# One stage of a streaming-encoder kernel: the conditioning product turned round, with the weights as the stationary side

## The chip, the cores and the metric

The kernel runs on one core of a Trainium2 chip. Such a core has a matrix engine (PE, with its weight loads shown apart as PEld), a vector engine (DVE), a scalar engine (ACT), a third elementwise engine (POOL) and a queue engine (SP) that issues the DMA transfers. Each engine works through its own list of instructions in order; semaphores tie the lists together. The metric is the device time of one execution in microseconds.

## The reference

One layer of an encoder takes a prompt of 4096 frames and a sample of 64 frames, 1024 features wide. Each of the two sequences has one conditioning vector `c`. What matters here is the head of the layer:

```python
mod = jnp.einsum('bd,de->be', c, w_ada) + b_ada
shift, scale, gate = jnp.split(mod, 3, axis=-1)
h = rms_norm(x, g_pre) * (1 + scale[:, None]) + shift[:, None]
p = jnp.einsum('btd,de->bte', h, w_in)
```

`w_ada` is 1024 x 3072, so the shift and the scale need its first 2048 columns, 8 MB in float32. They have to be known, for a block of 128 features, before that block of `h` can be formed, and `h` is what every projection with `w_in` reads. Behind the projections come two chunked recurrences (GLA and HGRN2, four heads each), a gate, an output projection and a last norm. All inputs and outputs are float32.

## The kernel before

The prompt is cut into 16 groups of 256 frames. Features lie on the partitions, in `KT` = 8 blocks of 128. To keep float32's accuracy in products of the faster `float32r` type, each operand is split into a high and a low part (`split`: ACT casts to `hi`, DVE subtracts to `lo`), and a product is made of three: high by high, high by low, low by high.

The change touches `first_group` (line 220), which works on group 0 while the weights still arrive. Its order is written by hand (`manual_schedule`); behind it a list scheduler places the instructions, so what stands there moves when something ahead of it changes. `first_group` does this:

- Six and then eight products of zeros run first (`warm`). The two tiles of x are normed and turned (`turn(0)`, `turn(1)`, line 313), and small rows (conditionings, biases, gains) are loaded into `rows` and turned into the columns of `col` (lines 302 and 325).
- For each of the eight blocks k, `ada_load` (line 207) issues four transfers of 256 KB: the columns of `w_ada` that give shift (e = 0) and scale (e = 1) of block k. `ada_split` cuts them into `ada_h` and `ada_l` (lines 93 and 94). `ada_sum` (line 239) multiplies them: the stationary side is `c4`, four columns (both conditionings, high and low), the moving side 256 columns of `ada_h` or `ada_l`. The sum has four rows and lies in bank `o` of PSUM; `ada_out` (line 249) copies it out by ACT, and `ada_turn` (lines 257 to 262) turns it by PE into columns and adds high, low and bias on DVE into `md`.
- `modulate` (lines 273 to 277) makes the parts of `h` for block k from `md`: ACT the high part `hh`, DVE the low one.
- The loop over k then takes twelve products for q and k (line 356, tiles `hh` and `wa`) and twelve for the gate z (line 625, tiles `wv` and `hh`). In iteration k, the sum for block k+1 stands behind the first eight of the q-k products, and `modulate(k+1)` behind the last four.
- The weights `w_in` come by `first_load`, in a tile `e` (q and k) and half a tile `wst` (z). `weights` loads and splits the next piece, `w_v` (tiles `wb`), of which every third low part is made by POOL.

Behind the first group come the products with `wb` (line 625), the exponentials of z (lines 1112 to 1114), the transposes of a small tile `at` (line 1129), the norm and transposes of group 1's x (lines 491, 496, 547) and group 1's q-k products (line 613).

Of the kernel before, what the change touches and what calls it, by code (L numbers as in the profile page):

```python
# [6 lines left out]
F32 = mybir.dt.float32  # L7
F32R = mybir.dt.float32r
# [20 lines left out]
class Kernel:  # L29
# [177 lines left out]
    def ada_load(self, ap, k, few=()):  # L207

        sts = []
        for i in range(2):  # L210
            st = ap.tile([P, 4, 2, P], F32, name="ada_st", bufs=5)
            for e in range(2):
                src = self.t["w_ada"][0, i * 512 : i * 512 + 512, e * D + k * P : e * D + (k + 1) * P]
                self.nc.sync.dma_start(st[:, :, e, :], src.rearrange("(n p) c -> p n c", p=P))
                for dst, src in few[2 * i + e : 2 * i + e + 1]:
                    self.nc.sync.dma_start(dst, src)
            sts.append(st)
        return sts

    def first_group(self, ap, ada, w, rows):  # L220


        nc, col = self.nc, self.col
        W = self.W1
        T = GROUP
        parts = {}

        def ada_split(st):
            hi = ap.tile([P, 4, 2, P], F32R, name="ada_h", bufs=3)
            lo = ap.tile([P, 4, 2, P], F32R, name="ada_l", bufs=3)  # L230
            self.split(hi, lo, st)
            return hi, lo

        def ada_sum(pa, parts, steps):


            for m, i in steps:
                for n in range(4):
                    nc.tensor.matmul(
                        pa, self.c4[:, 4 * i + n, :], parts[i][m][:, n],  # L240
                        start=m + i + n == 0, stop=(m, i, n) == (1, 1, 3),
                    )

        def ada_bank():
            return self.ps("o")[:4, : 2 * P]

        def ada_out(pa):
            am = self.etile()[:4, : 2 * P]
            nc.scalar.copy(am, pa)
            return am  # L250

        all_steps = [(0, 0), (0, 1), (1, 0), (1, 1)]

        def ada_turn(k, am):
            pt = self.ps("ms")
            for e in range(2):
                nc.tensor.transpose(pt[:, 4 * e : 4 * e + 4], am[:, e * P : (e + 1) * P], self.ident[:4, :4])
            md = self.md[:, :, k, :]
            nc.vector.tensor_reduce(
                md, pt[:, :8].rearrange("p (e m c) -> p e c m", e=2, m=2), mybir.AxisListType.X, ALU.add  # L260
            )
            nc.vector.tensor_tensor(
                md, md, col[:, 16:32].rearrange("p (e k) -> p e k", e=2)[:, :, k : k + 1].to_broadcast([P, 2, 2]), ALU.add
            )

        def gain(k):
            return col[:, 32 + k : 33 + k]

        def modulate(k):
            sh, gs = self.sh[:, k, :], self.gs[:, k, :]  # L270
            u = self.h0[k // 2][:, :, k % 2]
            hf = self.hf[k // 2][:, k % 2]
            nc.scalar.activation(u[:, 0], hf, AF.Identity, bias=sh[:, 0:1], scale=gs[:, 0:1])
            nc.vector.tensor_scalar(hf, hf, gs[:, 0:1], sh[:, 0:1], ALU.mult, ALU.add)
            nc.vector.tensor_tensor(u[:, 1], hf, u[:, 0].bitcast(F32), ALU.subtract)

            nc.vector.tensor_scalar(gs, gs, gain(k), None, ALU.mult)

        def raw(k, eng):

            dst, src = self.hf[k // 2][:, k % 2], pts[k // 2][:, k % 2]
            if eng is nc.scalar:
                nc.scalar.activation(dst, src, AF.Copy, scale=gain(k))
            else:
                nc.vector.tensor_scalar(dst, src, gain(k), None, ALU.mult)

        def w_split(i, w):
            W[("qk", "z")[i]].append(self.split_w(w[i], ("wa", "wv")[i]))

        zero = self.ep.tile([P, 512], F32R, name="zero", tag="e", bufs=5)  # L290
        nc.gpsimd.memset(zero.bitcast(F32), 0.0)
        ws, sts = [w], [ada, self.ada_load(ap, 1)]

        pqk = [self.ps("pj") for _ in range(2)]

        def warm(n):
            for _ in range(n):
                nc.tensor.matmul(pqk[0], zero[:, :P], zero, start=True, stop=True)

        warm(6)  # L300
        pr = self.ps("ms")
        nc.tensor.transpose(pr[:, :16], rows[:16], self.ident[:16, :16])
        warm(8)
        self.x_norm(0, [0])
        nc.vector.tensor_copy(col[:, :16], pr[:, :16])
        self.x_norm(0, [1])
        cT = col[:, 0:16].rearrange("p (s k) -> p k s", s=2)
        self.split(self.c4[:, :, 0:2], self.c4[:, :, 2:4], cT)
        pts = [self.ps(n).rearrange("p (k t) -> p k t", k=2) for n in ("tp", "at", "at", "pj")]

        def turn(j):
            for k in range(KT):
                nc.tensor.transpose(
                    pts[k // 2][:, k % 2, j * P : (j + 1) * P], self.xs[j][:, k * P : (k + 1) * P], self.ident
                )

        turn(0)
        pa = ada_bank()
        parts[0] = [ada_split(sts[0][0])]
        ada_sum(pa, parts[0], [(0, 0)])  # L320
        turn(1)
        parts[0].append(ada_split(sts[0][1]))
        ada_sum(pa, parts[0], [(0, 1)])
        pr = self.ps("ms")
        nc.tensor.transpose(pr[:, :52], rows, self.ident[:52, :52])
        ada_sum(pa, parts.pop(0), [(1, 0), (1, 1)])
        self.hf = [self.hp.tile([P, 2, T], F32, name="hf", bufs=4) for _ in range(4)]
        nc.vector.tensor_copy(col[:, 16:], pr[:, 16:52])
        nc.vector.tensor_scalar(col[:, 24:32], col[:, 24:32], 1.0, None, ALU.add)
        raw(0, nc.scalar)  # L330
        w_split(0, ws[0])
        am = ada_out(pa)
        ws.append(self.first_load(1))
        sts.append(self.ada_load(ap, 2))
        self.h0 = [self.hp.tile([P, 2, 2, T], F32R, name="hh", bufs=5) for _ in range(4)]
        ada_turn(0, am)
        modulate(0)
        parts[1] = [ada_split(st) for st in sts[1]]
        for i in range(1, KT):
            raw(i, nc.scalar if i < 4 else nc.vector)  # L340
        w_split(1, ws[0])
        pz = [self.ps(n) for n in ("pj", "at", "at", "tp")]
        for p in pqk:
            nc.tensor.matmul(p, zero[:, :P], zero, start=True, stop=False)
        vs = self.weights(W["v"], C_VA, 512, "wb", self.etile, 3)
        for k in range(KT):
            h = self.h0[k // 2][:, :, k % 2]
            hi, lo = h[:, 0], h[:, 1]
            if k + 2 < KT:
                ws.append(self.first_load(k + 2))  # L350
            u = W["qk"][k]

            def qk(bs, terms):
                for b in bs:
                    for i, x in terms:
                        nc.tensor.matmul(
                            pqk[b // 2][:, b % 2 * T : b % 2 * T + T], u[:, i, b * P : (b + 1) * P], x,
                            start=False, stop=k == KT - 1 and b % 2 == 1 and x is lo,
                        )

            qk((0, 1), [(0, hi), (1, hi)])
            if k + 1 < KT:
                for i in range(2):
                    w_split(i, ws[k + 1])
            qk((2, 3), [(0, hi), (1, hi)])
            if k + 1 < KT:
                pa = ada_bank()
                ada_sum(pa, parts.pop(k + 1), all_steps)
                am = ada_out(pa)
            qk(range(4), [(0, lo)])  # L370
            if k + 1 < KT:
                ada_turn(k + 1, am)
                modulate(k + 1)
            for j in range(2):
                for b in range(2):
                    self.tok_step(pz[2 * j + b], W["z"], 264 * b, 264 * b + 264, h, j * P, P, k)
            if k + 2 < KT:
                parts[k + 2] = [ada_split(st) for st in sts[k + 2]]
            if k + 3 < KT:
                sts.append(self.ada_load(ap, k + 3))  # L380
            if k == KT - 3:
                self.x_load(1, [0, 1])
            for _ in range(max(0, k - 4)):
                next(vs)
        self.vs0 = vs
        self.pre = [[p[:, i * T : i * T + T] for i in range(2)] for p in pqk] + [pz]
# [1414 lines left out]
```

## Time and profile before

| | |
|---|---|
| time of 3 runs, median | 2092.94 us |
| lowest and highest | 2091.45 and 2095.33 us |
| profiled execution: time | 2090.48 us |
| profiled execution: span | 2088.7 us |
| PE busy in it | 2045.3 us, 98% |
| DVE, ACT, POOL busy | 75%, 53%, 15% |

The span runs from the first to the last instruction; 1.8 us lie around it. In the timeline, a row gives the start, the length, the engine, the line, the operation, what is written and read, the shapes, how many of a kind follow each other, and in brackets how long the engine had been idle and who released it. "f32" also stands for `float32r` on PE. A float32 product appears as two loads and two products, a `float32r` product as one of each.

### The profile page before, as it was taken

The numbers are of one execution on the slowest core, as the hardware profiler recorded it, in microseconds if no ns is written. First come the engines' busy times: TensorE is split into PE (matmuls) and PEld (weight loads), VectorE is DVE, ScalarE is ACT, GpSimd is POOL, SyncE is SP. The second block draws the span as 40 slices with busy tenths as digits, with TensorE's granted clock in tenths as the row PEclk, the third lists the DMA queues.
The fourth block names the chain that finished last, engine by engine and source line by source line (L and its number), as shares of the span: only waits on it lengthen the run. The fifth ranks groups of instructions, "written<-read, shape, count | busy, mean of one in ns | idle before, by whom it ended". The sixth has DMA issues, their size and how long they took to land.

```text
span 2088.7 us, 47161 instructions
## 1 busy us (share of the span) xinstructions
PE 2045.3 (98%) x17384; PEld 1804.4 (86%) x17384; DVE 1559.2 (75%) x4795; ACT 1106.4 (53%) x3238; POOL 310.2 (15%) x781
## 2 busy tenths in 40 slices
PE   8999999999999999999999999999999999999998
PEld 6888899888899888999999999999987888888886
DVE  7777777676776687778888788778787776777775
ACT  6676666676666574444445444444445544433332
POOL 0111111111111211111111111111110002232321
PEclk9999999999999999999999999999999999999999
DMA  9322222222222242011111111111145764444443
GB/s 293 94 53 75 63 63 57 52 59 71 63 62 55 67 130 70 32 36 59 47 47 47 47 34 41 52 36 32 42 131 187 234 209 152 157 147 153 150 143 100
DMA packets 236116, 190.15 MB, mean 91 GB/s; under 512 B 138220, under 2 KB 160208, under 8 KB 235884
## 3 DMA queue, kind: packets, MB, share of 16 engines
q1 hardware_dynamic: 235740, 186.86, 29.9%
q8 instruction: 137, 2.24, 0.4%
q14 instruction: 95, 0.78, 0.1%
q10 hardware_dynamic: 144, 0.26, 0.0%
HBM read 126.60 MB, written 60.45 MB: 90 GB/s over the span
## 4 chain that ended last, share of the span: by engine, by line
PE 54%; DVE 8%; ACT 2%; DMA 1%; issue 1%; SPq 0%; DVEq 0%; POOL 0%; ACTq 0%
PE ps_pj L625 15%; PE ps_pj L613 13%; PE ps_pj L1403 13%; PE ps_o L1403 2%; DVE wst L967 2%; PE ps_at L1017 2%; PE ps_ms L819 2%; PE ps_o L798 2%; PE ps_o L803 1%; PE ps_at L693 1%; DMA wst<-in_w_in_dram 1%; DVE dd L699 1%; PE ps_pj L633 1%; PE ps_at L924 1%; PE ps_tp L773 1%; PE ps_at L1394 1%
## 5 line engine op out<-in xcount | busy, mean ns | idle before, releaser
L613 PE MATMUL ps_pj<-hh,wa 128*128 128x256 f32 (+1 forms) x2976 | 394.1, 288 | 3.1 <-ACT hh L93 3.1
L613 PEld LDWEIGHTS ps_pj<-hh,wa 128*128 128x128 f32 x2976 | 375.1, 192 | 7.9 <-ACT hh L93 3.4
L625 PE MATMUL ps_pj<-wb,hh 128*128 128x512 f32 x1536 | 379.4, 397 | 0.0
L625 PEld LDWEIGHTS ps_pj<-wb,hh 128*128 128x128 f32 x1536 | 279.9, 188 | 56.7 <-issue 2.7
L613 PE MATMUL ps_pj<-hh,wv 128*128 128x256 f32 (+1 forms) x1536 | 202.0, 286 | 0.0
L613 PEld LDWEIGHTS ps_pj<-hh,wv 128*128 128x128 f32 x1536 | 189.8, 188 | 8.7 <-issue 6.9
L625 PE MATMUL ps_pj<-wv,hh 128*128 128x264 f32 x1464 | 194.6, 288 | 0.1
L625 PEld LDWEIGHTS ps_pj<-wv,hh 128*128 128x128 f32 x1464 | 182.5, 188 | 4.3 <-ACT nwt_y L76 2.2
L625 PE MATMUL ps_pj<-wa,hh 128*128 128x512 f32 x768 | 177.9, 391 | 0.0
L625 PEld LDWEIGHTS ps_pj<-wa,hh 128*128 128x128 f32 x768 | 143.3, 188 | 30.7 <-issue 0.8
L1261 ACT ACTIVATE g<-ps_pj 128x256 f32<-128x256 f32 (+1 forms) x128 | 49.5, 387 | 216.2 <-PE ps_pj L613 215.8
L94 DVE TENSOR_TENSOR hh<-hf,hh 128x512 fp32r<-128x512 f32 (+1 forms) x188 | 128.9, 697 | 38.4 <-ACT hh L93 36.4
L93 ACT CAST hh<-hf 128x512 fp32r<-128x512 f32 (+1 forms) x188 | 117.3, 625 | 66.8 <-PE ps_pj L625 48.3
L998 POOL COPY T<-T 128x16 f32<-128x16 f32 (+1 forms) x32 | 7.9, 247 | 770.3 <-DVE Qg L859 431.9
L967 DVE TENSOR_TENSOR wst<-wst,T 128x160 f32<-128x160 f32 (+4 forms) x480 | 108.4, 266 | 1.1
L991 ACT ACTIVATE A<-Ac,member 128x128 f32<-128x128 f32 x256 | 80.4, 390 | 49.2 <-DVE Ac L985 49.2
L1463 ACT ACTIVATE sq<-e 128x512 bf16<-128x512 f32 x64 | 40.4, 631 | 119.7 <-DVE e L1475 119.7
L1403 PE MATMUL ps_pj<-wc,wa 128*128 128x512 f32 x384 | 98.5, 391 | 0.0
L1466 POOL TENSOR_TENSOR e<-e,gg 128x512 f32<-128x512 f32 x32 | 41.4, 1293 | 362.6 <-ACT sq L1463 352.0
L1403 PEld LDWEIGHTS ps_pj<-wc,wa 128*128 128x128 f32 x384 | 72.0, 188 | 16.1
L1000 POOL TENSOR_TENSOR T<-T,T 128x16 f32<-128x16 f32 (+1 forms) x224 | 82.5, 368 | 17.6
L830 DVE SCALAR_TENSOR_TENSOR S<-S,T,ps_ms 128x128 f32<-128x128 f32 x186 | 55.4, 343 | 34.7 <-PE ps_ms L819 34.7
(350 smaller groups left out, 4116.3 us busy)
## 6 DMA issues: line engine op xcount, KB each, us to landing
hf<-h_d SPq DMA_DIRECT2D x128, 256.0 KB
h_d<-hf SPq DMA_DIRECT2D x64, 256.0 KB
oh_d<-e SPq DMA_DIRECT2D x64, 256.0 KB
xq<-in_x_prompt_dram SPq DMA_DIRECT2D x64, 256.0 KB
out_y_prompt_dram<-xq SPq DMA_DIRECT2D x63, 256.0 KB
xt<-in_x_prompt_dram SPq DMA_DIRECT2D x448, 32.0 KB
wst<-in_w_in_dram SPq DMA_DIRECT2D x36, 256.0 KB
e<-oh_d SPq DMA_DIRECT2D x33, 256.0 KB
```

The lines of the kernel that those rows point to most:

```text
L93: self.nc.scalar.copy(hi, src)
L94: (eng or self.nc.vector).tensor_tensor(lo, src, hi.bitcast(F32), ALU.subtract)
L613: self.nc.tensor.matmul(ps[:, :T], a, b, start=i == 0, stop=i == n - 1)
L625: self.nc.tensor.matmul(ps[:r, : c1 - c0], a, b, start=kt == 0 and i == 0, stop=kt == KT - 1 and i == 2)
L798: nc.tensor.matmul(po[h], A[:, c * 4 + h, :], v, start=h < n, stop=St is None and h == 4 - n)
L819: nc.tensor.matmul(pd[s * w : (s + 1) * w, g, :], kc[:CL, g, s * w : (s + 1) * w], vs[c][:CL, h * P : (h + 1) * P], start=not apart, stop= ...
L830: nc.vector.scalar_tensor_tensor(Sn[:, g, :], St[:, g, :], T[:, c * G + g, 0:1], pd[:, g, :], ALU.mult, ALU.add)
L967: nc.vector.tensor_tensor(parts(dst), parts(src), t.unsqueeze(3).to_broadcast(shape), ALU.mult)
L991: nc.scalar.activation(Ah[:, :, 32 * b : 32 * b + 32], Ach, AF.Copy, scale=self.member[:CL, 8 + b : 9 + b])
L1000: nc.gpsimd.tensor_tensor(E8[:, :, i], E8[:, :, i - 1], T8[:, :, i], ALU.mult)
L1261: nc.scalar.activation(sg, pf[:, :T], AF.Sigmoid)
L1403: nc.tensor.matmul(bank, u[:, a, kt, :], W[name][kt][:, b], start=kt + i == 0, stop=kt + i == 5)
```

## The change

The sum is turned round. Each block of 128 x 128 of `w_ada` is now the stationary side as it was loaded, in float32, and the moving side is `cT`: two columns, one for each conditioning, in float32. A sum for block k is 2 (shift, scale) x 8 (blocks of the 1024 inputs) = 16 float32 products into two columns each. The results are columns at once, one bank for the shift (`o`) and one for the scale (`ms`), and two DVE instructions add the bias. The splits of `w_ada`, the copy and the two transposes per block are gone. The ring of staging tiles for `w_ada` has ten instead of five places. In the start, the transpose of the small rows now stands ahead of `turn(1)`, and the sum for block 0 stands in one piece behind both.

```diff
-            st = ap.tile([P, 4, 2, P], F32, name="ada_st", bufs=5)
+            st = ap.tile([P, 4, 2, P], F32, name="ada_st", bufs=10)
...
-        def ada_split(st):
-            hi = ap.tile([P, 4, 2, P], F32R, name="ada_h", bufs=3)
-            lo = ap.tile([P, 4, 2, P], F32R, name="ada_l", bufs=3)
-            self.split(hi, lo, st)
-            return hi, lo
-
-        def ada_sum(pa, parts, steps):
-            for m, i in steps:
+        cT = col[:, 0:16].rearrange("p (s k) -> p k s", s=2)
+
+        def ada_sum(pas, k, i):
+            for e in range(2):
                 for n in range(4):
                     nc.tensor.matmul(
-                        pa, self.c4[:, 4 * i + n, :], parts[i][m][:, n],
-                        start=m + i + n == 0, stop=(m, i, n) == (1, 1, 3),
+                        pas[e], sts[k][i][:, n, e], cT[:, 4 * i + n], start=i + n == 0, stop=i + n == 4
                     )
...
-        def ada_turn(k, am):
-            pt = self.ps("ms")
+        def ada_banks():
+            return [self.ps(n)[:, :2] for n in ("o", "ms")]
+
+        def ada_out(k, pas):
             for e in range(2):
-                nc.tensor.transpose(pt[:, 4 * e : 4 * e + 4], am[:, e * P : (e + 1) * P], self.ident[:4, :4])
...
+                nc.vector.tensor_scalar(
+                    self.md[:, e, k], pas[e], col[:, 16 + 8 * e + k : 17 + 8 * e + k], None, ALU.add
+                )
...
             if k + 1 < KT:
-                pa = ada_bank()
-                ada_sum(pa, parts.pop(k + 1), all_steps)
-                am = ada_out(pa)
+                pas = ada_banks()
+                ada_sum(pas, k + 1, 0)
+                ada_sum(pas, k + 1, 1)
             qk(range(4), [(0, lo)])
             if k + 1 < KT:
-                ada_turn(k + 1, am)
+                ada_out(k + 1, pas)
                 modulate(k + 1)
```

The start on PE, before (`ident,xt` are the eight transposes of one tile of x, `ident,rows` that of the small rows):

```order
L313 MATMUL ps_pj<-ident,xt 128x128 x2
L239 MATMUL ps_o<-ada_h,c_169 4x256 x4
L313 MATMUL ps_tp<-ident,xt 128x128 x2
L313 MATMUL ps_at<-ident,xt 128x128 x4
L313 MATMUL ps_pj<-ident,xt 128x128 x2
L239 MATMUL ps_o<-ada_h,c_169 4x256 x4
L325 MATMUL ps_ms<-ident,rows 128x52
L239 MATMUL ps_o<-ada_l,c_169 4x256 x8
```

The start on PE after the change, from the same eight transposes of the first tile on:

```order
L291 MATMUL ps_pj<-ident,xt 128x128 x2
L297 MATMUL ps_ms<-ident,rows 128x52
L291 MATMUL ps_tp<-ident,xt 128x128 x2
L291 MATMUL ps_at<-ident,xt 128x128 x4
L291 MATMUL ps_pj<-ident,xt 128x128 x2
L232 MATMUL ps_o<-col,ada_st 128x2 x4
L232 MATMUL ps_ms<-col,ada_st 128x2 x4
```

The first half of the sum no longer stands between the two tiles of x, and everything behind the transpose of the rows now waits for the last of these rows to arrive.

One iteration of the loop over k on PE, before (`hh,wa` are the q-k products, `ada_h,c` and `ada_l,c` the sum, `ident,e` the transposes of the sum):

```order
L356 MATMUL ps_pj<-hh,wa 128x256 x8
L239 MATMUL ps_o<-ada_h,c_169 4x256 x8
L239 MATMUL ps_o<-ada_l,c_169 4x256 x8
L356 MATMUL ps_pj<-hh,wa 128x256 x4
L257 MATMUL ps_ms<-ident,e 128x4 x2
L625 MATMUL ps_pj<-wv,hh 128x264 x3
L625 MATMUL ps_at<-wv,hh 128x264 x6
L625 MATMUL ps_tp<-wv,hh 128x264 x3
```

The same iteration after the change, where all lines behind `first_group`'s head have smaller numbers (329 for 356, 596 for 625):

```order
L329 MATMUL ps_pj<-hh,wa 128x256 x8
L232 MATMUL ps_o<-col,ada_st 128x2 x4
L232 MATMUL ps_ms<-col,ada_st 128x2 x4
L232 MATMUL ps_o<-col,ada_st 128x2 x4
L232 MATMUL ps_ms<-col,ada_st 128x2 x4
L329 MATMUL ps_pj<-hh,wa 128x256 x4
L596 MATMUL ps_pj<-wv,hh 128x264 x3
```

The sum keeps its place and its number of products, sixteen, with 2 moving columns instead of 256, and the transposes have left.

ACT behind the last `modulate`, before (`Xg`, `K_979` are the results of q and k, `wb` the high parts of `w_v`, `e<-ps_at` and the like the exponentials of z; the squares of group 1's x, line 491, stand ahead of this piece):

```order
L273 ACTIVATE hh<-hf,md 128x256
L93 CAST wb<-wst 128x512
L77 ACTIVATE nwt_y<-nwt_y 128x2
L93 CAST wb<-e 128x512
L1085 ACTIVATE Xg<-ps_pj 128x2x128
L93 CAST wb<-wst 128x512
L1085 ACTIVATE Xg<-ps_pj 128x2x128
```

After the change, the start of the same stretch, its middle, and its end:

```order
L252 ACTIVATE hh<-hf,md 128x256
L1056 ACTIVATE Xg<-ps_pj 128x2x128 x2
L93 CAST wb<-wst 128x512
L1066 COPY K_883<-ps_pj 128x2x128
L93 CAST wb<-e 128x512
L1066 COPY K_883<-ps_pj 128x2x128
```

```order
L93 CAST wb<-wst 128x512
L1083 ACTIVATE e<-ps_at 128x248
L1083 ACTIVATE e<-ps_pj 128x264
L93 CAST wb<-e 128x512
L1084 ACTIVATE e<-e 128x248
```

```order
L1085 ACTIVATE e<-e 128x264
L462 ACTIVATE hf,x_ss<-xt 128x1024 x2
L1152 COPY v<-ps_pj 128x512
L76 ACTIVATE nwt_y<-nwt_m 128x2
L77 ACTIVATE nwt_y<-nwt_y 128x2
```

The scheduler has moved the first casts of `w_v` behind the two copies of q, the last of them behind two exponentials, and the squares of group 1's x behind all exponentials; the two small instructions that finish the root of the norm (lines 76 and 77) stand behind the first copy of the `wb` products out of PSUM (line 1152). On PE, 34 products with `wb` instead of 25 stand ahead of the first transpose of `at`, and the transposes of group 1's x stand behind all 48.

More of the change, by code (lines that the diff above doesn't have):

```diff
@@ L225, in first_group @@
         T = GROUP
-        parts = {}
-        def ada_split(st):
-            hi = ap.tile([P, 4, 2, P], F32R, name="ada_h", bufs=3)
-            lo = ap.tile([P, 4, 2, P], F32R, name="ada_l", bufs=3)
-            self.split(hi, lo, st)
-            return hi, lo
-        def ada_sum(pa, parts, steps):
-            for m, i in steps:
+        cT = col[:, 0:16].rearrange("p (s k) -> p k s", s=2)
+        def ada_sum(pas, k, i):
+            for e in range(2):
                 for n in range(4):
                     nc.tensor.matmul(
-                        pa, self.c4[:, 4 * i + n, :], parts[i][m][:, n],
-                        start=m + i + n == 0, stop=(m, i, n) == (1, 1, 3),
-                    )
[L244 to L252, printed above, removed]
-        def ada_turn(k, am):
-            pt = self.ps("ms")
-            for e in range(2):
[L257 to L264, printed above, removed]
+                        pas[e], sts[k][i][:, n, e], cT[:, 4 * i + n], start=i + n == 0, stop=i + n == 4
+                    )
+        def ada_banks():
+            return [self.ps(n)[:, :2] for n in ("o", "ms")]
+        def ada_out(k, pas):
+            for e in range(2):
+                nc.vector.tensor_scalar(
+                    self.md[:, e, k], pas[e], col[:, 16 + 8 * e + k : 17 + 8 * e + k], None, ALU.add
+                )
         def gain(k):
@@ L306, in first_group @@
         self.x_norm(0, [1])
-        cT = col[:, 0:16].rearrange("p (s k) -> p k s", s=2)
         self.split(self.c4[:, :, 0:2], self.c4[:, :, 2:4], cT)
@@ L317, in first_group @@
         turn(0)
-        pa = ada_bank()
[L319 to L323, printed above, removed]
         pr = self.ps("ms")
         nc.tensor.transpose(pr[:, :52], rows, self.ident[:52, :52])
-        ada_sum(pa, parts.pop(0), [(1, 0), (1, 1)])
+        turn(1)
         self.hf = [self.hp.tile([P, 2, T], F32, name="hf", bufs=4) for _ in range(4)]
@@ L331, in first_group @@
         w_split(0, ws[0])
-        am = ada_out(pa)
+        pas = ada_banks()
+        ada_sum(pas, 0, 0)
+        ada_sum(pas, 0, 1)
         ws.append(self.first_load(1))
@@ L335, in first_group @@
         self.h0 = [self.hp.tile([P, 2, 2, T], F32R, name="hh", bufs=5) for _ in range(4)]
-        ada_turn(0, am)
+        ada_out(0, pas)
         modulate(0)
-        parts[1] = [ada_split(st) for st in sts[1]]
         for i in range(1, KT):
@@ L366, in first_group @@
             if k + 1 < KT:
-                pa = ada_bank()
-                ada_sum(pa, parts.pop(k + 1), all_steps)
-                am = ada_out(pa)
+                pas = ada_banks()
+                ada_sum(pas, k + 1, 0)
+                ada_sum(pas, k + 1, 1)
             qk(range(4), [(0, lo)])
             if k + 1 < KT:
-                ada_turn(k + 1, am)
+                ada_out(k + 1, pas)
                 modulate(k + 1)
@@ L376, in first_group @@
                     self.tok_step(pz[2 * j + b], W["z"], 264 * b, 264 * b + 264, h, j * P, P, k)
-            if k + 2 < KT:
-                parts[k + 2] = [ada_split(st) for st in sts[k + 2]]
             if k + 3 < KT:
```

## The prediction

> **What bounds the kernel now.** I read the page first, then PE's timeline of the first group, then the timelines of DVE, ACT and POOL there. The page says that PE is the bound almost everywhere:
>
> ```profile
> span 2088.7 us, 47161 instructions
> PE 2045.3 (98%) x17384; PEld 1804.4 (86%) x17384; DVE 1559.2 (75%) x4795; ACT 1106.4 (53%) x3238; POOL 310.2 (15%) x781
> ```
>
> So time lost or won on PE at the start stays in the end, unless a later wait of PE shrinks. The profiled execution took 2090.48 us; the median of the runs is 2092.94, 2.5 us above it. I work out a difference from the profile and add it to the median. A measurement of this kernel can tell about 0.2% from no change, 4.2 us; that is the bound for "faster" and "slower" here.
>
> The change lies in the first 64 us. PE there: the first iteration's start, one whole iteration (k = 2), the start of the last, and the first product behind the group:
>
> ```profile
> 16.37 1.22 PE L356 MATMUL ps_pj<-hh,wa 128*128 128x256 f32 x8 [0.50 <-ACT hh L273]
> ...
> 30.34 1.11 PE L356 MATMUL ps_pj<-hh,wa 128*128 128x256 f32 x8
> 31.29 1.21 PE L239 MATMUL ps_o<-ada_h,c 128*4 128x256 f32 x8
> 32.34 0.62 PE L239 MATMUL ps_o<-ada_l,c 128*4 128x256 f32 x4
> 33.32 0.63 PE L239 MATMUL ps_o<-ada_l,c 128*4 128x256 f32 x4 [0.37 <-DVE ada_l L94]
> 33.79 0.64 PE L356 MATMUL ps_pj<-hh,wa 128*128 128x256 f32 x4
> 34.41 0.28 PE L257 MATMUL ps_ms<-ident,e 4*128 4x4 f32 x2
> 34.62 0.63 PE L625 MATMUL ps_pj<-wv,hh 128*128 128x264 f32 x3
> ...
> 36.17 1.11 PE L356 MATMUL ps_pj<-hh,wa 128*128 128x256 f32 x8
> ...
> 60.81 1.60 PE L356 MATMUL ps_pj<-hh,wa 128*128 128x256 f32 x12
> ...
> 63.72 6.12 PE L625 MATMUL ps_pj<-wb,hh 128*128 128x512 f32 x25
> ```
>
> An iteration takes 36.17 - 30.34 = 5.83 us, and PE is idle in it for only 0.37 us. The seven iterations up to the last take 60.81 - 16.37 = 44.4 us, 6.35 each, since some meet longer waits. The sum (line 239) takes 33.79 - 31.29 = 2.50 us of the 5.83. The 0.37 us belongs to a ring of waits that runs through the other engines:
>
> ```profile
> 34.73 0.17 DVE L259 TENSOR_REDUCE md<-ps_ms 128x4 f32<-128x8 f32 x1 [0.24 <-PE ps_ms L257]
> 35.13 0.60 ACT L273 ACTIVATE hh<-hf,md 128x256 fp32r<-128x256 f32 x1 [0.78 <-DVE md L262]
> 35.63 1.99 ACT L93 CAST ada_h<-ada_st 128x1024 fp32r<-128x1024 f32 x2
> 36.70 2.36 DVE L94 TENSOR_TENSOR ada_l<-ada_st,ada_h 128x1024 fp32r<-128x1024 f32 x2
> ```
>
> `md` at 34.73 releases ACT's high part, then DVE's low parts and then the splits of `w_ada`, 1.99 us on ACT and 2.36 us on DVE per block. The last split ends at 39.06, and the next sum waits for it. So two bounds lie close together: PE's work, and this ring.
>
> **What the change removes.** The splits go: per block 1.99 us of ACT and 2.36 us of DVE. That opens the ring, and the 0.37 us goes with it. The transposes go too, 34.62 - 34.41 = 0.21 us of PE per block, and the 256-column products of the sum. DVE's two additions replace a reduction and an addition of the same small size, which I count as nothing.
>
> **What it adds on PE.** Sixteen float32 products per block, each of which has to load 128 x 128 weights. Nothing in the trace loads so much for two columns. These rows bound the price (loads and products of two heads, line 798, where two float32 products stand as four records; the product behind them; the group of such loads with the mean length of one; then the same for the loads of the old transposes):
>
> ```profile
> 117.68 0.52 PEld L798 LDWEIGHTS ps_o<-v,A 128*128 128x128 f32 x4 [0.69 <-ACT sq L838]
> 117.68 0.71 PE L798 MATMUL ps_o<-v,A 128*128 128x128 f32 x4 [0.37 <-ACT sq L838]
> 118.33 0.71 PE L803 MATMUL ps_o<-S,Qg 64*128 64x128 f32 x4
> L798 PEld LDWEIGHTS ps_o<-v,A 128*128 128x128 f32 x384 | 51.5, 190 | 23.7 <-ACT A L936 19.1 <-ACT sq L838 3.3
> 28.55 0.19 PEld L257 LDWEIGHTS ps_ms<-ident,e 4*128 4x128 f32 x2 [0.24 <-ACT e L249]
> L257 PEld LDWEIGHTS ps_ms<-ident,e 4*128 4x128 f32 x16 | 1.6, 135 | 2.8 <-ACT e L249 2.8
> ```
>
> Four loads take 0.52 us, and one is 0.19 us long, so (0.52 - 0.19) / 3 = 0.11 us pass from load to load. A product streams while the next load runs (both rows start at 117.68), so with two columns the load alone sets the pace. A block needs 16 x 2 = 32 loads: 32 x 0.11 = 3.55 us, against 2.50 + 0.21 = 2.71 before. From below, the two loads at 28.55 (0.19 us together, one 0.135, each for a transpose of four rows) stand 0.055 to 0.06 us apart: 1.9 us per block. From above, the group at 117.68 is followed by the next kind of product at 118.33, 0.65 us for four, 0.16 each: 5.2 us per block. I take 0.11, because those loads have the type, the full 128 rows and the 128 columns of the new ones.
>
> The page "FP8 and Floating Point Precision" of the Trainium skill (section "TensorE Precision Notes") counts four passes through the array for a true FP32 product. If each pass had its own load, a block would need 64 loads, 7.0 us, and the kernel would be some 25 us slower still; the trace's two loads for a product speak against it.
>
> **The sum, up to the end of the first group.** An iteration then has 12 q-k products at 0.119 (0.95 us for eight), the z products, 36.17 - 34.62 = 1.55, and 3.55 for the sum: 6.53 us. Behind the sum stand 0.48 + 1.55 = 2.0 us of products, and `md` to `hh` takes 35.73 - 34.41 = 1.3, so that chain hides. The data is there in time: a block is 1 MB of `w_ada` and 0.53 MB of `w_in`, and this window moves 303 GB/s:
>
> ```profile
> 30.00:40.00 10.00, 9.28 (x75) 7.22 (x73) 8.99 (x16) 6.99 (x11) 0.00 (x0) 1.00 1.06 303
> ```
>
> That is 1.58 MB / 303 GB/s = 5.2 us per block, less than 6.53, and the ring of ten places removes waits of the queue that no longer matter. Seven iterations: 45.7 us instead of 44.4, **+1.3 us**.
>
> The start moves as well. The rows that decide it:
>
> ```profile
> 9.71 0.25 SPq L198 DMA_DIRECT2D rows<-in_g_onorm_hgrn_dram  x1
> 12.91 0.26 PE L325 MATMUL ps_ms<-ident,rows 52*128 52x52 f32 x1
> ```
>
> The last small row is issued at 9.71 to 9.96 and is in use at 12.91; I take its arrival as 12.4 (no earlier than 10, no later than 12.9). `w_ada`'s first block is no later: the old order multiplied both its halves ahead of the row at 12.91. So PE has its transposes done at about 12.4 + 0.9 = 13.3, the whole sum at 16.9 instead of spread between the transposes, and the first `hh` 1.2 us later: 18.1 instead of 16.37, **+1.7 us**. The last iteration (63.72 - 60.81 = 2.9) has no sum and stays. The group ends at R = 66.7 instead of 63.72: **+3.0 us**.
>
> **Behind the group.** Freed ACT and DVE could give time back here, since PE now waits for them. Before:
>
> ```profile
> 52.94 1.06 ACT L491 ACTIVATE hf<-xt 128x1024 bf16<-128x1024 f32 x1 [1.20 <-DMA xt<-in_x_prompt_dram]
> 62.21 0.38 ACT L1085 ACTIVATE Xg<-ps_pj 128x256 f32<-128x256 f32 x1 [0.71 <-PE ps_pj L356]
> 66.99 1.49 POOL L94 TENSOR_TENSOR wb<-e,wb 128x512 fp32r<-128x512 f32 x1
> 69.80 0.38 ACT L1112 ACTIVATE e<-ps_at 128x248 f32<-128x248 f32 x1 [3.28 <-DVE wb L94]
> 72.40 0.31 PE L1129 MATMUL ps_ms<-ident,at 128*80 128x128 f32 x1 [2.56 <-DVE at L1124]
> 74.07 0.60 PE L547 MATMUL ps_tp<-ident,xt 128*128 128x128 f32 x4
> 80.43 4.73 PE L613 MATMUL ps_pj<-hh,wa 128*128 128x256 f32 x36
> 110.03 0.49 PE L798 MATMUL ps_o<-v,A 128*128 128x128 f32 x2 [0.96 <-ACT A L936]
> ```
>
> The squares of group 1's x (1.06 us each) lay inside the first group at 52.94; in the new order they stand behind all exponentials. I walk ACT's new list with lengths of the rows above, counted from R. The copies of q can start 1.5 us ahead of R, as at 62.21, and now hold the first cast of `w_v` behind them; eight casts of 512 columns (0.5 us each, half of one at 35.63) would end near R + 3, but the last one stands behind two exponentials, which wait for a tile `e` until DVE has split the sixth piece, near R + 6.4 (69.80 is R + 6.1). So POOL gets its last piece at R + 7.7 and needs 1.5 to 1.6 us (66.99), and the exponentials for the second tile wait for that until R + 9.4. In order behind them on ACT is what `at` needs: PE can transpose it at R + 11.2, where it was R + 8.7 (72.40). PE's 34 products before it last until about R + 8.3 (25 take 6.12 at 63.72), so PE waits 2.9 us there, not 2.6. The other exponentials end at R + 12.4, the squares at R + 14.6. The norm's root then stands behind a copy that needs all 48 products, done at R + 14.6; the copy (512 columns, 0.5), some small steps (1) and DVE's scaling of two tiles of 1024 columns (I take 1.8; two instructions of that size take 2.36 at 36.70) make about R + 18 for x's transposes, an estimate; they were at R + 10.4 (74.07). PE has nothing else from R + 15.9 on. Group 1's q-k products start at R + 19.7 (1.5 us for the first modulation and cast) instead of R + 16.7 (80.43), and are fed by ACT pair by pair, some 1 us more; four transposes (0.4) are already done. That makes +3.6. Later waits of PE, such as the 0.96 us at 110.03, should give about 1 back: **+2.6 us**.
>
> Sum: 1.3 + 1.7 + 2.6 = +5.6 us, and 2092.9 + 5.6 = **2098.5 us**. With the bounds of the load price, the loop alone goes from 7 x 5.2 - 44.4 = -8.0 (the transfers then bind) to 7 x 8.2 - 44.4 = +13; the part behind the group from -1.5 (no wait for ACT or DVE left, 2.6 us less, but 1 us of feeding) to +5.
>
> **Rivals.** *Cheap loads* (faster). If loads for two columns follow each other as at 28.55, an iteration is 1.43 + 1.55 + 1.9 = 4.9 us of PE, and the transfers bind at 5.2: -8.0 in the loop, nothing in the start, +2.6 behind: 2087.5 us. It decides from below 0.09 us per load, where 32 loads cost what the old sum did. Against it: every load of 128 columns for a product in the rows above has the longer length. *The queues behind the group clear* (same). DVE's splits of `w_v` can use the 2.4 us per block that it won, and the walk above has many steps; then R + 3.0 stays and the part behind gives back 1 to 2: 2094.5. For it speaks that PE waited 2.6 us at 72.40 behind a busy DVE. Against it, ACT's order. *The clock gate* (slower still). A wait of 3.14 us lowered the granted clock to 0.50:
>
> ```profile
> 710.57 0.90 PE L613 MATMUL ps_pj<-hh,wa 128*128 128x320 f32 x2 [3.14 <-ACT hh L93]
> 710.00:715.00 5.00, 4.43 (x17) 4.39 (x18) 5.00 (x10) 2.70 (x5) 3.45 (x1) 0.50 0.58 142
> ```
>
> The waits near R + 8.3 and R + 15.9 are almost as long, and PE's array does next to nothing in a sum of 3.55 us. One such stretch of 5 to 7 us at half speed costs about 3.4 us; if the sums themselves count as idle, several follow: 2102 to 2118. The page "TensorE: Matmul & The Clock Gate" of the Trainium skill (section "What's actually happening") has a window of about 3.4 us after which an idle array falls to half its clock; the row at 710.57 agrees with it, and no row shows whether loads with two columns count as idle. That the change doesn't do what it says is excluded: the new order shows sixteen products per block and no split.
>
> **How the numbers follow.** Forecast 0.48 (its own range 2095.5 to 2101.5), cheap loads 0.14, queues clear 0.28, clock gate 0.10. Faster by over 0.2% (below 2088.8) is most of the cheap loads: 0.12. Slower (above 2097.1) is three quarters of the forecast, the clock gate and a little of the rest: 0.48. Within 0.2%: 0.40. The range leaves out the cheaper half of the cheap loads and the upper part of the clock gate: 2089 to 2105.
>
> **What would show it.** In the new timeline, four loads of a sum should stand 0.44 us from the next four, an iteration should take 6.5 us with PE without idle time, and the first `wb` product should start near 66.7. The splits' 36 us of DVE and ACT should be missing without any gain in the loop. x's transposes should start near R + 18 with a wait of about 2 us ahead of them. Wrong is the forecast if the loads stand 0.06 apart, if iterations are paced by transfers, or if group 1's q-k products start no more than 17 us behind R.

## The result, and the profile after

The changed kernel is slower: 2120.30 us (median of 4 runs, 2118.38 to 2121.48) against 2092.19 us for the kernel before on the same chip; the ratio is 1.0131, with a 95% interval from 1.0118 to 1.0144. The forecast was 2098.5 us and the range ended at 2105. What happened is the rival with the chance of 0.10, the clock gate, and a little more of it than its own upper end, 2118.

The page of the changed kernel, its first part and the granted clock by slices:

```profile
span 2118.4 us, 47316 instructions
PE 2079.2 (98%) x17496; PEld 1848.2 (87%) x17496; DVE 1539.4 (73%) x4779; ACT 1087.8 (51%) x3214; POOL 310.7 (15%) x781
...
PEclk7799999999999999999999999999999999999999
```

DVE and ACT have lost 20 and 19 us, as the change meant. PE is busy for 34 us more, and the first two slices of the clock, some 53 us each, read 7 instead of 9. The same windows of 10 us that stood at clock 1.00 before (columns: busy time and records of PE, PEld, DVE, ACT and POOL, then the granted clock, the DMA share and GB/s):

```profile
20.00:30.00 10.00, 10.00 (x45) 9.34 (x45) 5.02 (x13) 3.25 (x7) 0.00 (x0) 0.50 1.16 318
30.00:40.00 10.00, 10.00 (x62) 10.00 (x62) 2.94 (x9) 2.59 (x5) 0.00 (x0) 0.67 1.12 311
...
90.00:100.00 10.00, 9.14 (x43) 7.01 (x41) 7.92 (x18) 7.69 (x22) 4.88 (x7) 1.00 0.25 72
```

In the window from 30 to 40 us PE was "busy" for 9.28 us with 75 records before, and for 10.00 us with 62 records now. Busy time doesn't show the clock; the count of records and the clock do. PE's timeline has the start, one iteration (k = 3), the start of the last one and what follows the group:

```profile
12.51 0.23 PE L297 MATMUL ps_ms<-ident,rows 52*128 52x52 f32 x1 [1.46 <-DMA rows<-in_g_onorm_hgrn_dram]
...
13.60 1.33 PE L232 MATMUL ps_o<-col,ada_st 128*128 128x2 f32 x8
...
21.05 2.08 PE L329 MATMUL ps_pj<-hh,wa 128*128 128x256 f32 x8
...
24.49 1.85 PE L232 MATMUL ps_ms<-col,ada_st 128*128 128x2 f32 x8
26.20 1.85 PE L232 MATMUL ps_o<-col,ada_st 128*128 128x2 f32 x8
...
51.14 1.30 PE L329 MATMUL ps_pj<-hh,wa 128*128 128x256 f32 x8
52.28 0.95 PE L232 MATMUL ps_o<-col,ada_st 128*128 128x2 f32 x8
53.09 1.03 PE L232 MATMUL ps_ms<-col,ada_st 128*128 128x2 f32 x8
53.98 1.03 PE L232 MATMUL ps_o<-col,ada_st 128*128 128x2 f32 x8
...
87.12 2.48 PE L329 MATMUL ps_pj<-hh,wa 128*128 128x256 f32 x12
...
90.90 8.29 PE L596 MATMUL ps_pj<-wb,hh 128*128 128x512 f32 x34
100.30 0.31 PE L1100 MATMUL ps_ms<-ident,at 128*80 128x128 f32 x1 [1.10 <-DVE at L1095]
...
105.75 0.30 PE L518 MATMUL ps_tp<-ident,xt 128*128 128x128 f32 x1 [1.11 <-DVE xt L467]
...
108.75 0.50 PE L584 MATMUL ps_pj<-hh,wa 128*128 128x256 f32 x2
```

Eight loads stand 0.89 us apart at full clock (53.09 to 53.98), 0.11 each, as priced; at 24.49 they stand 1.71 us apart, 0.21 each. Seven iterations take 87.12 - 21.05 = 66.1 us, 9.4 each instead of 6.5. The group ends at R = 90.90 us, 27.2 us later than before; the span ends 29.7 us later. So the time went in the ramp, nearly all of it.

### The profile page after: what moved, and what is told of

The parts are those of the page before. It is cut to its first block, busy times and chain, and to the rows that moved or that the text cites. A ratio compares the mean times of both kernels' runs of the same rounds, so it can differ in the third digit from the quotient of the medians.

```text
span 2118.4 us, 47316 instructions
## 1 busy us (share of the span) xinstructions
PE 2079.2 (98%) x17496; PEld 1848.2 (87%) x17496; DVE 1539.4 (73%) x4779; ACT 1087.8 (51%) x3214; POOL 310.7 (15%) x781
## 3 DMA queue, kind: packets, MB, share of 16 engines
q1 hardware_dynamic: 235740, 186.86, 29.7%
## 4 chain that ended last, share of the span: by engine, by line
PE 54%; DVE 7%; ACT 1%; DMA 1%; issue 1%; SPq 0%; DVEq 0%; POOL 0%; ACTq 0%
PE ps_pj L596 16%; PE ps_pj L584 13%; PE ps_pj L1374 13%; PE ps_o L1374 2%; DVE wst L938 2%; PE ps_at L988 2%; PE ps_ms L790 2%; PE ps_o L769 2%; PE ps_o L774 1%; PE ps_at L664 1%; DMA wst<-in_w_in_dram 1%; PE ps_pj L604 1%; DVE dd L670 1%; PE ps_at L895 1%; PE ps_tp L744 1%; PE ps_at L1365 1%
```

## The experiments

Two theories: **A**, the sums lower the clock because two columns leave the array next to idle while the loads run; **B**, the float32 loads as such (their type or their number), or the later start, lower it. The clock of the changed kernel is recorded in pieces of 3.41 us. Laid on these pieces, its windows read (PE's busy time and records, then clock, DMA share, GB/s):

```profile
31.08:34.49 3.41, 3.41 (x17) 0.50 1.09 325
34.49:37.91 3.42, 3.42 (x33) 1.00 1.13 321
37.91:41.32 3.41, 3.41 (x17) 0.50 1.18 304
41.32:44.73 3.41, 3.41 (x18) 0.50 0.68 191
44.73:48.15 3.42, 3.42 (x32) 1.00 1.10 311
48.15:51.56 3.41, 3.41 (x18) 0.50 1.03 398
51.56:54.97 3.41, 3.41 (x32) 1.00 0.06 23
```

Between 10.6 and 89.1 us 16 of 23 pieces are at 0.50. Behind the 1.46 us for the last small row (12.51) PE waits for nothing there, and a piece at half clock has half as many records. That first wait lies in the piece from 10.60 us on, and the next piece is already at 0.50, so the clock first fell in the start, where the sum had only begun (13.60).

### More columns on the moving side

```diff
+        cw = ap.tile([P, KT, 128], F32, name="cw", bufs=1)
+        nc.gpsimd.memset(cw, 0.0)
...
+        nc.vector.tensor_copy(cw[:, :, 0:2], cT)
...
-   pas[e], sts[k][i][:, n, e], cT[:, 4 * i + n], start=i + n == 0, stop=i + n == 4
+   pas[e], sts[k][i][:, n, e], cw[:, 4 * i + n], start=i + n == 0, stop=i + n == 4
```

The second run has 32 in place of 128.

> The changed kernel with 128 columns on the moving side of each product of the sums, the two conditionings and 126 columns of zeros; the loads, their number, their order and the start are those of the change. The two theories. A: the sums lower the granted clock because two columns per pair of loads leave the array next to idle for 3.55 us out of 6.5. B: float32 loads (or their number, or the later start) lower it, whatever moves. A expects a granted clock of 1.0 from the first sum to the end of the first group, iterations of about 6.5 us, the end of the first group at 67 us of the span instead of 90.9, and 2095 to 2100 us in all, the prediction's own sum. B expects the changed kernel's time or a little more, 2120 to 2124 us, with the granted clock still at 0.5 for most of the ramp.

> As the run with 128 columns, but with 32: a product moves for a quarter of the time, its two loads last as before. A, read strictly (anything that moves counts), expects 2095 to 2100 us; A, read as a share of time in which the array multiplies, expects something between that and the changed kernel's 2120 us, with pieces of 3.4 us at clock 0.5 left in the ramp. B expects 2120 us.

Measured: 2103.87 us with 128 columns, ratio 1.0048 [1.0031, 1.0065]; 2111.09 us with 32, 1.0083 [1.0062, 1.0104]. B is excluded as the main cause: the same loads with more columns of zeros behind them run 16 us faster. But 128 columns miss the 2095 to 2100 that A gave. The timeline of that run says where:

```profile
13.24 0.69 PE L294 MATMUL ps_tp<-ident,xt 128*128 128x128 f32 x2
...
27.85 1.11 PE L332 MATMUL ps_pj<-hh,wa 128*128 128x256 f32 x8
28.80 1.05 PE L232 MATMUL ps_o<-cw,ada_st 128*128 128x128 f32 x8
29.69 1.06 PE L232 MATMUL ps_ms<-cw,ada_st 128*128 128x128 f32 x8
...
34.32 1.11 PE L332 MATMUL ps_pj<-hh,wa 128*128 128x256 f32 x8
...
63.22 2.08 PE L332 MATMUL ps_pj<-hh,wa 128*128 128x256 f32 x8 [2.89 <-ACT hh L252]
```

An iteration takes 34.32 - 27.85 = 6.47 us, the predicted 6.53. Two other things cost: the clock fell ahead of the first sum already, after the wait for the small rows (the transposes at 13.24 are at half clock), and the scheduler had put the norm of group 1's rows on DVE ahead of an addition of the sum, so that PE waited 2.89 us and the clock fell again.

With 32 columns some pieces are at 0.50 and some are not (PEclk 0.50, 0.67, 0.83, 0.69, 0.80 in the windows from 20 to 70 us). So it isn't "anything moves" against "nothing moves"; a share counts.

### Two columns, mixed with other products; and half a sum

```diff
+            more = iter(())
+            if k + 1 < KT:
+                pas = ada_banks()
+                more = ada_steps(pas, k + 1)
...
                             start=False, stop=k == KT - 1 and b % 2 == 1 and x is lo,
                         )
+                        next(more, None)
...
-                ada_sum(pas, k + 1, 0)
-                ada_sum(pas, k + 1, 1)
...
+            for _ in more:
+                pass
```

`ada_steps` issues the products of `ada_sum` one at a time. The second run is the change without its second half of each sum:

```diff
-                ada_sum(pas, k + 1, 1)
```

> The changed kernel with the sixteen products of a sum put one behind each of the twelve q-k products of the iteration before, and four behind the last; two columns still, the same loads, no product more or less. A expects that the long idle stretch is what counts and that it is gone: clock near 1.0, iterations of about 6.5 us, 2095 to 2101 us. If instead a mixed stretch (0.11 us of multiplying to each 0.22 us of loads) counts as idle too, the time stays near 2115 us. B expects 2120 us.

> The changed kernel with half of each sum left out (the second 512 of the 1024 rows of w_ada are not multiplied, so the shift and the scale are those of the first 512): eight products, sixteen loads, 1.78 us at full clock instead of 3.55 us. A expects that a stretch of 1.78 us never fills one of the 3.41 us pieces in which the clock is set: clock 1.0, iterations of about 4.8 us, the end of the first group near 54 to 57 us, and 2082 to 2088 us. B, and a form of A in which the share of idle time over several microseconds counts (1.78 of 4.8), expect pieces at 0.5 still, iterations of 6 us or more, and 2095 us or more.

Measured: mixed 2129.14 us, ratio 1.0172 [1.0156, 1.0187], worse than the change; half a sum 2087.95 us, 0.9968 [0.9958, 0.9979]. Half a sum bears out A where the clock had recovered: from 27.45 to 75.24 us it is at 1.00 and an iteration takes 4.70 us, where B expected 6 us or more.

```profile
27.82 1.12 PE L328 MATMUL ps_pj<-hh,wa 128*128 128x256 f32 x8
...
32.52 1.11 PE L328 MATMUL ps_pj<-hh,wa 128*128 128x256 f32 x8
```

From 13.80 to 27.45 us, behind a wait of 2.41 us for the small rows, that clock was at 0.50 all the same, which A had not expected, and the group ended at 58.79 us instead of 54 to 57.

The mixed run is a miss for both theories as they stood. Its timeline at full clock:

```profile
47.84 0.37 PE L333 MATMUL ps_pj<-hh,wa 128*128 128x256 f32 x1
48.05 0.28 PE L232 MATMUL ps_o<-col,ada_st 128*128 128x2 f32 x2
48.19 0.37 PE L333 MATMUL ps_pj<-hh,wa 128*128 128x256 f32 x1
```

A pair takes 0.35 us, of which a q-k product's 256 columns stream 0.12. That is a third, over a stretch of 5 us, so no piece inside it reaches more; in the change the same products stand in a row, and the pieces that hold them are well filled. If a piece's share decides, mixing spreads the shortfall over nearly every piece.

That led to a count over all runs of this study and both kernels. The share of a piece is the time that the columns of its product records need at full clock, over 3.41 us. A column is 0.46 ns: the 22 products of 512 columns in the row at 67.82 us further down take (5.30 - 0.39) / 21 = 0.234 us each, where 0.39 is the length of one. The columns of a record are spread evenly over its length, and a record of a float32 product of the sums counts twice. In the first 125 us of the twelve executions 411 pieces have a recorded successor. With one bound at 0.41, 408 of them have the right successor: below it the next piece is at 0.50, above it at 1.00, and the three others lie between 0.40 and 0.42. If float32 records count once, the best bound leaves 17 wrong, with four 8. For the seven pieces shown above the shares are 0.55, 0.10, 0.41 (0.407), 0.44, 0.07, 0.56 and 0.24, and what follows each of them is 1.00, 0.50, 0.50, 1.00, 0.50, 1.00 and 0.50. (Where the expectations say 0.37, a column was taken as 0.42 ns.) This rule was found in the first four of these runs; the next ones test it. In the six executions behind them (204 of the 411 pieces, 15 with 0.50 behind them) it has no piece wrong.

The rule is shown for these 125 us only. Carried on to 2060 us the same count has 20 of 7215 pieces wrong, 17 of them between 700 and 830 us, where shares of 0.29 to 0.40 are followed by 1.00 and shares of 0.41 to 0.73 by 0.50. Other float32 products and products that write only 32 rows stand in some of these pieces, and the count may weigh them wrongly; that is open.

### The rule tested, with the two disturbances taken out

```diff
         turn(0)
+        warm(12)
...
+            if k == KT - 1:
+                self.x_norm(1, [0, 1])
...
-                    self.x_norm(g, [0, 1])
```

With this, the moving side has 128, 64 or 2 columns; the fourth run is the kernel before with the norm alone placed so. In all four the squares of group 1's x also go into a tile `e` instead of `hf`.

> 128 columns on the moving side, with two disturbances of the first run of that kind taken out: twelve products of zeros stand in TensorE's queue where it waited for the last of the small rows, and the norm of group 1's rows is placed by hand behind the last iteration instead of where the scheduler put it (in front of the sixth sum's additions, where PE then waited 2.89 us). The theory now, with its threshold: the clock of a piece of 3.41 us is set by the share of the piece before in which columns were streaming, 0.5 below about 0.37 and 1.0 above. It expects a clock of 1.0 from the first sum to the end of the first group, the first q-k products at 18 us, iterations of 6.46 us as in the undisturbed part of the first run, the end of the group near 66 us, and 2092 to 2098 us in all. The rival, that the loads or their type cost as such, expects no gain on the first run of 128 columns beyond the 6 us of the two disturbances.

> The same with 64 columns: a sum now streams for 0.48 of its time (64 columns at 2.4 columns per ns and two passes per load are 0.053 us of the 0.11). The threshold of 0.37 expects no difference from 128 columns: clock 1.0 throughout, iterations of 6.46 us, the same time within 1 us. If any shortfall of streaming counts in proportion, pieces of 0.5 come back, and the time lies between the 128 columns' and 2111 us.

> The changed kernel's two columns, with the same two repairs (products of zeros ahead of the small rows, the norm of group 1's rows placed by hand). If the dip of the clock before the first sum, or the place of the norm, made the loss, this runs like the one with 128 columns, 2092 to 2098 us. The threshold theory expects the first piece at 0.5 as soon as the first sum has filled one, the ramp at 0.5 for about two thirds of the time as in the change, the end of the group at 84 to 90 us, and 2112 to 2120 us.

> The kernel before with the norm of group 1's rows placed by hand as in these runs (behind the last iteration of the first group), so that the runs with it have their own reference. The clock is 1.0 there already, so the theories agree: the end of the first group stays at 64 us; the transposes of x for group 1 can come a few us earlier than 74 us, which the queue behind them may or may not pass on: 2088 to 2094 us.

Measured, against the kernel before on that chip (2094.58 us): 128 columns 2102.73 us, ratio 1.0034 [1.0021, 1.0047]; 64 columns 2104.69 us, 1.0044 [1.0027, 1.0061]; two columns 2114.14 us, 1.0091 [1.0071, 1.0111]; the kernel before with the norm placed by hand 2097.19 us, 1.0015 [1.0006, 1.0025].

In the ramp the rule holds: iterations of 6.47 us with 64 and 6.46 us with 128 columns, and no piece at 0.50 from the first sum to the end of the group; with two columns, the old picture, 14 of 22 pieces at 0.50 between 11.2 and 86.3 us. (With 64 columns one piece falls behind the group, from 70.98 us on, after a wait of 1.92 us.) Rows of the timeline with 64 columns, then the windows with two:

```profile
25.39 1.11 PE L333 MATMUL ps_pj<-hh,wa 128*128 128x256 f32 x8
26.34 1.00 PE L232 MATMUL ps_o<-cw,ada_st 128*128 128x64 f32 x8
...
31.86 1.11 PE L333 MATMUL ps_pj<-hh,wa 128*128 128x256 f32 x8
```

```profile
10.00:20.00 10.00, 10.00 (x61) 0.90 1.02 295
20.00:30.00 10.00, 10.00 (x47) 0.50 1.16 318
30.00:40.00 10.00, 10.00 (x63) 0.67 1.15 316
```

So the start and the norm's place made only a part of the loss: without them two columns still stand 19.6 us above the kernel before, against 28.1 us in the change, and 11.4 us above 128 columns in the same order.

The totals missed their ranges, 2092 to 2098 for the wide ones; the two repairs together gained the run with 128 columns only 1.1 us. Its first q-k products came at 19.92 us instead of 18, PE waited 0.47, 0.84 and 0.73 us for pieces of `wb` behind the group, and placing the norm by hand cost the kernel before 2.6 us instead of nothing. That last has to be taken off: 128 columns stand 2102.73 - 2097.19 = 5.5 us above their own reference, not 8. The medians of 64 and 128 columns are 2 us apart, the two profiled executions 5.7 us (the one with 128 is the fastest of its five), and these don't come from the ramp. Up to 715 us the trace with 64 columns is up to 1.3 us ahead; at 800 us it is 4.4 us behind, and it has four pieces at 0.50 between 719 and 761 us, the other one:

```profile
710.00:725.00 15.00, 10.44 (x45) 0.82 0.38 101
...
755.00:770.00 15.00, 15.00 (x98) 0.82 0.42 132
```

```profile
710.00:725.00 15.00, 10.43 (x48) 0.89 0.39 110
...
755.00:770.00 15.00, 15.00 (x108) 1.00 0.52 160
```

The kernel before has two such pieces near 711 us. Which products fall into which piece changes with every shift ahead of them, and in these traces that goes with some microseconds of the whole.

### The change without the fall of the clock

```diff
         turn(0)
+        warm(10)
...
+        cw = ap.tile([P, KT, 64], F32, name="cw", bufs=1)
```

As the run with 64 columns, but the norm stays where the scheduler puts it, which is behind the first group here.

> 64 columns on the moving side and ten products of zeros ahead of the small rows, and nothing placed by hand: the scheduler leaves the norm of group 1's rows behind the first group, as in the kernel before and in the change. So this is the change with the clock's fall taken out and nothing else, and tests the prediction's own sum. The threshold theory expects clock 1.0 through the ramp, the first q-k products at 18 to 19 us (16.4 before), iterations of 6.46 us, the end of the group at 67 us (63.7 before), what lies behind it 1 to 3 us later still, and 2095 to 2100 us in all, 0.15 to 0.35% above the kernel before. If something beside the clock costs in the change (its additions on VectorE from a bank of PSUM, its later loads), the time stays above 2103 us as in the first run with 128 columns.

Measured: 2094.56 us (11 runs), ratio 1.0012 [1.0003, 1.0021]; the span is 2091.7 us, 3.0 above the kernel before. Two of its windows, laid on the pieces, and its timeline:

```profile
26.73:30.14 3.41, 3.41 (x33) 1.00 1.10 319
30.14:33.55 3.41, 3.41 (x32) 1.00 1.08 319
```

```profile
18.56 1.22 PE L333 MATMUL ps_pj<-hh,wa 128*128 128x256 f32 x8 [0.48 <-ACT hh L252]
...
25.12 1.11 PE L333 MATMUL ps_pj<-hh,wa 128*128 128x256 f32 x8
...
31.59 1.11 PE L333 MATMUL ps_pj<-hh,wa 128*128 128x256 f32 x8
...
63.90 1.59 PE L333 MATMUL ps_pj<-hh,wa 128*128 128x256 f32 x12
...
67.82 5.30 PE L600 MATMUL ps_pj<-wb,hh 128*128 128x512 f32 x22 [0.87 <-ACT Xg L1060]
75.23 0.31 PE L1104 MATMUL ps_ms<-ident,at 128*80 128x128 f32 x1 [2.12 <-DVE at L1099]
...
76.19 0.60 PE L522 MATMUL ps_tp<-ident,xt 128*128 128x128 f32 x4
```

There are 32 or 33 records in these pieces, as in the change's pieces at full clock, and every piece up to 712 us is at 1.00. The fall of the clock, its first fall in the start included, thus costs the change some 26 of its 28 us, and the product turned round costs 2.4 us by itself (0.0012 x 2092; the interval reaches from 0.6 to 4.4). That is just below the 2095 to 2100 us expected, because what lies behind the group did not come later still; the table further down has the terms.

### The first sum ahead of the small rows

```diff
         turn(0)
-        warm(10)
+        pas = ada_banks()
+        ada_sum(pas, 0, 0)
+        turn(1)
...
         nc.tensor.transpose(pr[:, :52], rows, self.ident[:52, :52])
-        turn(1)
+        ada_sum(pas, 0, 1)
```

The transpose of the small rows writes bank `pj` here, since `ms` holds a half of the sum.

> As the last run (64 columns, nothing placed by hand), but without the products of zeros, and with the first block's sum split as the kernel before has it: its first half behind the first row tile's transposes, ahead of the small rows, its second half behind them. It tests the term of the start. If the sum's place behind the last small row is what makes the start late (18.56 us in the last run against 16.37 us before), the first q-k products come at 15.8 to 16.5 us, the end of the group 2 to 2.5 us earlier than in the last run, near 65 us, and the time is 2091.5 to 2094 us, within 0.1% of the kernel before; what is left is the loop's 0.9 us. If the start is set by the loads of w_ada or of the first block's q-k weights instead, the first q-k products stay at 18 us and the time at 2094.5 us. If the clock's rule fails here (no zeros any more in the wait for the rows), a piece of 0.5 shows before 20 us.

Measured: 2091.94 us (12 runs) against 2095.02 us, ratio 0.9990 [0.9981, 0.9999].

```profile
13.52 0.26 PE L303 MATMUL ps_pj<-ident,rows 52*128 52x52 f32 x1 [0.20 <-DMA rows<-in_g_onorm_hgrn_dram]
...
16.77 1.22 PE L332 MATMUL ps_pj<-hh,wa 128*128 128x256 f32 x8 [0.54 <-ACT hh L252]
```

The first q-k products come at 16.77 us, 1.8 us earlier than in the last run, though the small rows were transposed later here (13.52 instead of 12.77); the 15.8 to 16.5 us expected were just missed. No piece falls to 0.50 in the ramp. It is the best version of the change: level with the kernel before, or a hair faster; the interval ends just below 1, and the traces of the two stand within 0.5 us of each other at 650 us, so I don't call it faster.

## Why the prediction was wrong

**The step that failed** is "with two columns the load alone sets the pace": right as a price per load at full clock, and wrong in taking that clock for granted through a sum in which almost nothing streams. The sum of +5.6 us has no term for the clock. The pieces above show the price (0.11 us) and the clock (0.50 in 16 of 23 pieces) side by side. Sixteen pieces of 3.41 us at half clock cost at most 16 x 3.41 / 2 = 27 us of work; the group ended 90.90 - 66.7 = 24.2 us later than forecast. The rival had named the mechanism, "if the sums themselves count as idle", and 0.10 was too little for it: the window of 3.4 us and a sum of 3.55 us stood in the same text.

The other steps, on the run with 64 columns and nothing placed by hand, where the clock stays at 1.00:

| term | predicted | measured | from |
|---|---|---|---|
| one load | 0.11 us | 0.11 us | 53.09 to 53.98, change |
| an iteration | 6.53 us | 6.47 us | 25.12 to 31.59 |
| loop | +1.3 us | +0.9 us | 63.90 - 18.56 against 44.44 |
| start | +1.7 us | +2.2 us | 18.56 against 16.37 |
| last iteration | 0 | +1.0 us | 67.82 - 63.90 against 63.72 - 60.81 |
| behind the group | +2.6 us | -1.1 us | 3.0 of span less 4.1 |
| sum | +5.6 us | +3.0 us | spans 2091.7 and 2088.7 |

- **Loop and start** were right within half a microsecond. In the change the sum started at 13.60; with 3.55 us for it and 1.2 us to the first `hh` that would have been 18.35, against the 18.1 forecast; it was 21.05 because the sum took 6.3 us. The cause of the later start, the first sum's place behind the last small row, is shown by the run that moves half of it.
- **The last iteration** was said to stay. In the run with 64 columns the first `wb` product waits 0.87 us for ACT's copy of q (67.82), which is most of the 1.0 us: there ACT's eight casts of `w_v` (62.87 to 67.1 us) stand ahead of that copy. In the change, whose order the forecast walked, they stand behind it and PE doesn't wait (90.90).
- **Behind the group** the forecast walked ACT's list to R + 11.2 for `at`, R + 18 for x's transposes and R + 19.7 for group 1's q-k products. In the change they stand at R + 9.4, R + 14.9 and R + 17.9, and the span ends 29.7 - 27.2 = 2.5 us later than R alone says, beside the 2.6 forecast. Each point was put 1.8 to 3.1 us late, and the agreement of the 2.5 is partly chance, since a piece at 0.50 (109.6 to 113.0 us) is in it. With 64 columns the scheduler orders this part otherwise, x's transposes stand at 76.19, which is R + 8.4, and the term has turned into a gain. So this term belongs to one order of the list, not to the product.
- **The queues behind the group clear**, the rival with 2094.5, has the time that the run without the fall of the clock came to, 2094.56. The agreement is in the total: there R is 4.1 us later, not 3.0, and whether DVE's free time made the 1.1 us behind it is not shown.
- **Cheap loads** is excluded by the 0.11 us.
- The bounds of the range were worked out from the load's price, and the clock's rival was cut off at its upper part. The clock was the larger unknown: no row of the kernel before had a stretch of loads with two columns, and that should have opened the range to the rival's 2118 at least; the 2120.30 measured lies above even that.

## What to carry to other kernels

A product with a few moving columns has the price of its weight loads only while the array has enough to stream from other products; several such products in a row, 3.4 us long, can halve the clock of everything around them (16 of 23 pieces here), and mixing them evenly with other work can be worse than keeping them apart (2129 against 2120 us). Where loads set the pace, columns of zeros on the moving side were free up to the time of the load here (64 and 128 columns both ran at 0.11 us a load) and kept the clock up; 32 columns were too few. Read the granted clock of the stage, not PE's busy time, and look for other stages near the bound before a shift of a few microseconds is explained by anything else.

## What the runs showed of the hardware

- In the first 125 us of these executions the clock of a piece of 3.41 us follows from the piece before it, in 408 of 411 cases: at 1.00 if columns streamed for more than about 0.41 of it, else at 0.50. The page "TensorE: Matmul & The Clock Gate" of the Trainium skill (section "What's actually happening") has a free-running window of 3.4 us and the two states, and the pieces here agree. It speaks of idle and busy windows; the rows here show windows in which PE is busy throughout (3.42 of 3.42 us from 44.73 on, at 1.00), with loads back to back, and behind which the clock is at 0.50 all the same.
- At half clock a filled piece comes to a share of only about 0.55 (0.56 at most), so that by the bound of 0.41 about three quarters of the piece must stream to get the clock back. That fits the mixed run, which has a third in its pairs and stayed at 0.50 for 34 us on end.
- The kernel before is itself near the bound: its piece from 13.5 us on, in the start, has a share of 0.42.
- The two records of a float32 product of the sums have to count twice each for one bound to fit, which makes four passes per product. The page "FP8 and Floating Point Precision" of the Trainium skill (section "TensorE Precision Notes") has four as well; the trace has two loads per product, so by this count two passes share a load.
